# Token tiles 0 and 1 through w_v without their norm, the factor put on v's rows

## The chip, the cores and the metric

The kernel runs on one core of one Trainium2 chip. The metric is the device time of one execution in microseconds (us). The core's engines are TensorE (PE: matmuls and transposes), VectorE (DVE), ScalarE (ACT), GpSimd (POOL) and SyncE (SP, which issues most DMAs). Each engine works through its own queue in order; semaphores order them among each other.

## The reference

One residual block over 1024 tokens of width 1024, in float32:

```python
def rmsnorm(x, g):
    y = xf * lax.rsqrt(jnp.mean(xf * xf, axis=-1, keepdims=True) + RMS_EPS)
    return (y * g.astype(jnp.float32)).astype(x.dtype)

h = rmsnorm(x, norm_mix_pre[l])
m = mixer(h, w_in[l], b_f[l], conv_w[l], w_branch[l], w_out[l])
x = x + rmsnorm(m, norm_mix_post[l])
h = rmsnorm(x, norm_ffn_pre[l])
f = swiglu(h, w_gate_up[l], w_down[l])
x = x + rmsnorm(f, norm_ffn_post[l])
```

The mixer projects h by w_in onto q, k, v, a forget logit and the inputs of a gated convolution and of two gates. It merges a short convolution with an attention that has a bias from the forget gates, and projects by w_out. The change concerns h = rmsnorm(x) and v = h · w_v, with the eight forget logits as eight more columns of w_v. The factor 1/sqrt(mean(x²) + eps) of the norm is one number per token, so per row of h and of v; the gain g is one number per column of h.

## The kernel before

The tokens are cut into eight tiles of 128. For each tile the kernel loads x, takes the sum of squares on ACT, the factor on POOL (`rms_scale`: an addition `va` and a power `r1`), and scales x (`hn`). PE turns the tile by eight 128x128 transposes into two PSUM tiles `tp` (tag `mm`, four buffers). The turned columns are split into a rounded high part and a low remainder (`hB11h`, `hB11l` and so on): ACT copies to the rounded type, DVE subtracts. A product is three matmuls, high by high, high by low, low by high, so v of a tile is 2 column halves x 8 k-slices x 3 = 48 matmuls of 260 columns into PSUM (`pv`, two buffers). `v_out` copies v out of PSUM on ACT and stores it by a POOL DMA.

The projections behind it are products of the Strassen kind on a 2x2 cut of h. Its four blocks are `hB11` (tokens 0 to 511, k-slices 0 to 3), `hB21` (same tokens, k-slices 4 to 7), `B12` and `hB22` (tokens 512 to 1023). Tiles 4 to 7 therefore make four sums each on DVE (`t12`, `t34`) from their own turned columns and those of tiles 0 to 3, which are kept unsplit in `hraw`; two 1024-column splits (`hT12`, `hT34`) follow.

In the head of the kernel all engines keep program order (`strict`), so the order is written out by hand (lines 425 to 531). Between the first loads and the first products PE runs matmuls on a tile of zeros (`spins`). Tiles 0 and 1 (`Scaled`) are normed without the gain, turned, and get the gain as a column factor `gcol` when `hraw` is written; their v accumulates slice by slice as the slices of w_v arrive (`Parts`, with `wv_high` and `wv_low` splitting a slice). From tile 2 on the gain is in the norm (`gm`). From line 533 on tiles 2 to 7 run in a loop, whose order on DVE, ACT and POOL is set by a scheduler. DMA issues are part of their queue's order too: SP issues the loads of x and w_v, each of x's three buffers is loaded again when its last reader is done.

Of the kernel before, what the change touches and what calls it, by code (L numbers as in the profile page):

```python
# [10 lines left out]
F32 = mybir.dt.float32  # L11
# [35 lines left out]
def block_kernel(  # L47
# [58 lines left out]
    def f32(ap):  # L106
        return ap.bitcast(F32)
# [10 lines left out]
    def copy(o, a):  # L118
        nc.scalar.activation(o, a, AF.Copy)
# [42 lines left out]
    nc.vector.memset(ones, 1.0)  # L162
# [8 lines left out]
    pad(stat, 112, "pad_s")  # L171
# [6 lines left out]
    def st_tile(name, w=1):  # L178
        return stat.tile([P, w], F32, tag=name, name=name)
# [57 lines left out]
    strict[0] = engines  # L237
    gm = ax.tile([P, D], F32, name="gm")
# [9 lines left out]
    nc.scalar.activation(warm, ones[:, 0:1], AF.Square)  # L248
# [11 lines left out]
    zero = ap.tile([P, 4, P], F32R, tag="b12h", name="zero", bufs=2)  # L260
    nc.vector.memset(f32(zero), 0.0)
# [22 lines left out]
    def norm_sum(st):  # L284

        xt = xq.popleft()
        hn = ap.tile([P, D], F32, tag="hn", name="hn", bufs=2)
        ssq = st_tile("ssq")
        nc.scalar.activation(hn, xt, AF.Square, scale=ROOT, accum_out=ssq)
        return xt, hn, ssq  # L290

    def norm_rest(st, xt, hn, rs):

        nc.vector.scalar_tensor_tensor(hn, xt, rs, gm, op0=ALU.mult, op1=ALU.mult)
        if st + 3 < ST:
            xq.append(load_x(st + 3))
        return hn
# [5 lines left out]
    def turned(hn):  # L303

        tps = []
        for q in range(2):
            tp = psa.tile([P, 4, P], F32, tag="mm", name="tp")
            for k in range(4):
                kt = 4 * q + k
                nc.tensor.transpose(tp[:, k, :], hn[:, kt * P : (kt + 1) * P], ident)  # L310
            tps.append(tp)
        return tps
# [3 lines left out]
    class Scaled:  # L316


        def __init__(self, st):
            self.ss = slice(st * P, (st + 1) * P)  # L320
            self.ops = [tuple(t[:, :, self.ss] for t in b) for b in (hB11, hB21)]

# [3 lines left out]
        def turn(self, hn):  # L326
            self.tps = turned(hn)
# [97 lines left out]
    xt = xq.popleft()  # L425
    hn = ap.tile([P, D], F32, tag="hn", name="hn", bufs=2)
    s2, part = st_tile("s2", 2), st_tile("nm")
    for n, c in enumerate((n1, n2)):
        nc.scalar.activation(
            hn[:, c], xt[:, c], AF.Square, scale=ROOT, accum_out=s2[:, n : n + 1]  # L430
        )
        if n == 0:
            nc.vector.tensor_scalar(part, s2[:, 0:1], EPS, None, op0=ALU.add)
    rs0 = rms_scale(s2[:, 1:2], part)
    nc.vector.tensor_scalar(hn[:, n1], xt[:, n1], rs0, None, op0=ALU.mult)
    nc.scalar.activation(hn[:, n2], xt[:, n2], AF.Identity, scale=rs0)
    nc.vector.tensor_copy(gcol, gps)
    xq.append(load_x(3))
    t0, t1 = Scaled(0), Scaled(1)
    t0.turn(hn)  # L440
    spins(4)
    xt1, hn1, ssq1 = norm_sum(1)
    wv_high(0)
    t0.scale(0)
    t0.high(0)

    def between():
        t0.scale(1)
        t0.low(0)

    rs1 = rms_scale(ssq1, between=between)
    v0, v1 = Parts(t0.ops), Parts(t1.ops)
    v0.run("hh", 0)
    spins(1)
    wv_high(1)
    v0.run("hh", 1)
    v0.run("lh", 0, 1)
    t0.high(1)
    nc.vector.tensor_scalar(hn1[:, n1], xt1[:, n1], rs1, None, op0=ALU.mult)
    nc.scalar.activation(hn1[:, n2], xt1[:, n2], AF.Identity, scale=rs1)  # L460
    xq.append(load_x(4))
    spins(1)
    t1.turn(hn1)
    wv_low(0)
    wv_high(2)
    v0.run("hh", 2)
    v0.run("lh", 2)
    v0.run("hl", 0)
    wv_high(3)
    t0.low(1)  # L470
    v0.run("hh", 3)
    v0.run("lh", 3)
    wv_high(4)
    t1.scale(0)
    t1.high(0)
    wv_low(1)
    v0.run("hh", 4)
    v0.run("lh", 4)
    v0.run("hl", 1)
    wv_high(5)  # L480
    t1.low(0)
    t1.scale(1)
    v1.run("hh", *range(4))
    v1.run("lh", *range(4))
    wv_high(6)
    wv_low(2)
    t1.high(1)
    v1.run("hl", 0, 1)
    t1.low(1)
    wv_high(7)  # L490
    wv_low(3)
    for k in (2,):
        v0.run("hl", k)
        v1.run("hl", k)
    v0.run("hh", 5)
    v0.run("lh", 5)
    xt2, hn, ssq2 = norm_sum(2)
    v0.run("hl", 3)
    v1.run("hl", 3)
    wv_low(4)  # L500
    v0.run("hh", 6)
    v0.run("lh", 6)
    sum3 = norm_sum(3)

    def between():
        for k in (5, 6, 7):
            wv_low(k)

    rs2 = rms_scale(ssq2, between=between)
    v1.run("hh", 4, 5)  # L510
    v1.run("lh", 4, 5)
    v0.run("hl", 4)
    v1.run("hl", 4)
    norm_rest(2, xt2, hn, rs2)
    v0.run("hh", 7)
    v0.run("lh", 7)
    v1.run("hh", 6)
    v1.run("lh", 6)
    v0.run("hl", 5, 6, 7)
    rs3 = rms_scale(sum3[2])  # L520
    v_out(0, v0.pv)
    v1.run("hh", 7)
    v1.run("lh", 7)
    v1.run("hl", 5, 6)
    cur = turn(2, hn)
# [1793 lines left out]
```

## Time and profile before

| what | value |
|---|---|
| median of 3 runs | 1318.18 us (1317.93 to 1319.31) |
| profiled execution | 1319.89 us |
| span of the profiled execution | 1318.0 us |
| PE busy | 1308.8 us (99% of the span) |
| DVE busy | 917.2 us (70%) |
| ACT busy | 555.8 us (42%) |
| POOL busy | 185.6 us (14%) |

Times in the profile count from the start of the span. The chain that ended last is followed back from the last instruction through what released each step; its pieces say where the time of the end is made. A row of the timeline has its start, its length, the engine, the line, and the operation with its tiles; the brackets behind it say how long the engine had been idle and what ended that. A matmul's length is modelled and includes its way through the array, so the distance between starts says how fast PE goes. Most operations are recorded on one helper line (L76), so groups are told apart by tiles.

### The profile page before, as it was taken

How to read it: one execution, taken by the hardware profiler on the slowest of the kernel's cores; microseconds unless marked ns; L12 is line 12 of the kernel's file. 1: busy time of each engine (PE TensorE's matmuls, PEld its weight loads, DVE VectorE, ACT ScalarE, POOL GpSimd, SP SyncE). 2: the span in 40 equal slices, each digit the busy share in tenths (PEclk: the TensorE clock that was granted, in tenths of full speed). 3: DMA queues.
4: the chain of work that ended last, by engine and by line, in shares of the span. 5: the costliest groups of instructions: out<-in, count | busy, mean ns of one | idle time of the engine just before them, and what ended most of it. 6: DMA issues, size and time to landing. Idle time of an engine off the chain costs nothing.

```text
span 1318.0 us, 17686 instructions
## 1 busy us (share of the span) xinstructions
PE 1308.8 (99%) x6695; PEld 1089.3 (83%) x6695; DVE 917.2 (70%) x1313; ACT 555.8 (42%) x869; POOL 185.6 (14%) x347
## 2 busy tenths in 40 slices
PE   9999999999999999999999999999999999999998
PEld 8988888888888888888888888888888888888886
DVE  6883768776756866676667788866766666677674
ACT  6631323243355766513678432222322234344451
POOL 3101001012112212011223112111001110000001
PEclk9999999999999999999999999999999999999999
DMA  6352423556536445674476565533323337966551
GB/s 225 90 160 88 141 61 119 183 194 195 196 128 206 154 138 166 210 257 132 131 231 227 174 198 193 176 120 104 99 86 115 110 106 271 364 217 192 159 169 64
DMA packets 168389, 215.71 MB, mean 164 GB/s; under 512 B 11480, under 2 KB 113952, under 8 KB 168304
## 3 DMA queue, kind: packets, MB, share of 16 engines
q1 hardware_dynamic: 146352, 141.40, 34.5%
q0 software_dynamic: 21952, 73.19, 15.3%
q8 instruction: 52, 0.85, 0.3%
q14 instruction: 33, 0.27, 0.1%
HBM read 153.41 MB, written 61.15 MB: 163 GB/s over the span
## 4 chain that ended last, share of the span: by engine, by line
PE 96%; ACT 1%; DVE 1%; DMA 1%; issue 1%; POOL 0%; DVEq 0%; POOLq 0%; SPq 0%; ACTq 0%
PE b L76 61%; PE pd L76 16%; PE pv L76 4%; PE pbb L76 3%; PE pba L76 3%; PE po L76 2%; PE tps L76 2%; PE sp L76 2%; PE tp L76 1%; PE ma L76 1%; PE mb L76 1%; DMA raw<-in_w_gate_up_dram 0%; ACT raw L76 0%; DMA xt<-in_x_dram 0%; DVE x L76 0%
## 5 line engine op out<-in xcount | busy, mean ns | idle before, releaser
L76 DVE TENSOR_TENSOR c<-c,b 128x512 f32<-128x512 f32 x215 | 146.8, 683 | 96.9 <-PE b L76 87.4
L76 DVE TENSOR_TENSOR lo<-raw,hi 128x1024 fp32r<-128x1024 f32 (+1 forms) x91 | 109.7, 1205 | 81.2 <-PE b L76 65.7
L76 ACT ACTIVATE hi<-raw 128x1024 fp32r<-128x1024 f32 (+1 forms) x98 | 99.7, 1017 | 102.0 <-PE b L76 68.5
L76 ACT ACTIVATE hi<-sx 128x1024 fp32r<-128x1024 f32 x44 | 46.8, 1063 | 207.2 <-PE b L76 181.3
L76 DVE TENSOR_TENSOR lo<-sx,hi 128x1024 fp32r<-128x1024 f32 x44 | 53.8, 1223 | 39.6 <-PE b L76 37.9
L76 PE MATMUL b<-w12h,lo 128*128 128x512 f32 x208 | 80.9, 389 | 0.0
L76 PE MATMUL b<-w12h,hi 128*128 128x512 f32 x204 | 79.4, 389 | 0.0
L76 PE MATMUL b<-w12l,hi 128*128 128x512 f32 x204 | 79.4, 389 | 0.0
L76 PE MATMUL b<-hh,hi 128*128 128x512 f32 x176 | 69.0, 392 | 0.0
L76 PE MATMUL b<-hh,lo 128*128 128x512 f32 x176 | 68.5, 389 | 0.0
L76 PE MATMUL b<-hl,hi 128*128 128x512 f32 x176 | 68.5, 389 | 0.0
L76 DVE TENSOR_TENSOR sx<-raw 128x512 f32<-128x512 f32 x78 | 53.6, 687 | 20.0 <-DMA raw<-in_w_in_dram 10.3
L76 PE MATMUL b<-w,s4h 128*128 128x512 f32 x208 | 64.0, 389 | 0.0
L76 PE MATMUL pd<-hi,lo 128*128 128x512 f32 x160 | 62.3, 389 | 0.0
L76 PE MATMUL pd<-hi 128*128 128x512 f32 x160 | 61.9, 390 | 0.0
L76 PE MATMUL pd<-ghi 128*128 128x512 f32 x148 | 57.6, 389 | 0.0
L76 PE MATMUL pd<-ghi,glo 128*128 128x512 f32 x148 | 57.6, 389 | 0.0
L76 PE MATMUL pd<-glo,ghi 128*128 128x512 f32 x148 | 57.6, 389 | 0.0
L76 POOL DMA_DIRECT2D a_dramA<-um x33 | 17.9, 541 | 276.6 <-DVE um L76 275.8
L76 PE MATMUL b<-hT34h,hi 128*128 128x512 f32 x136 | 53.0, 390 | 0.4 <-DVE c L76 0.4
L76 PE MATMUL b<-hT34h,lo 128*128 128x512 f32 x136 | 52.9, 389 | 0.0
L76 PE MATMUL b<-hT12h,hi 128*128 128x512 f32 x136 | 52.9, 389 | 0.0
(451 smaller groups left out, 3572.8 us busy)
## 6 DMA issues: line engine op xcount, KB each, us to landing
raw<-in_w_gate_up_dram SPq DMA_DIRECT2D x52, 512.0 KB, 3.8
raw<-in_w_in_dram SPq DMA_DIRECT2D x35, 512.0 KB, 3.8
a_dramS<-um POOLq DMA_DIRECT2D x44, 256.0 KB, 3.1
a_dramA<-um POOLq DMA_DIRECT2D x33, 256.0 KB, 2.6
sg<-sg_dram SPq DMA_DIRECT2D x32, 256.0 KB, 4.2
graw<-a_dramS SPq DMA_DIRECT2D x14, 512.0 KB, 4.3
sg_dram<-c POOLq DMA_DIRECT2D x24, 256.0 KB, 2.5
raw<-in_w_down_dram SPq DMA_DIRECT2D x11, 512.0 KB, 4.4
```

The lines of the kernel that those rows point to most:

```text
L76: ins = getattr(self.engine, name)(*args, **kw)
```

## The change

Tiles 0 and 1 are turned as they were loaded (`First`, in place of `Scaled`), the gain is put on with `gcol` as before, and the products with w_v are made from these columns, whose rows lack the norm's factor. The factor is put on when v is copied out of PSUM (`v_out(..., scale=firsts[t].rs)`). The squares of tiles 0 and 1 come later in the order, and the order of the head is written as a string of steps (`wh`, `wl`: high and low part of a slice of w_v; `x`, `s`, `h`, `l`: transposes, gain, high and low part of half a tile; `phh13`: high by high for tile 1, slice 3; `sq`, `pw`: square and power). `settle`, behind v of tile 2, puts the two factors on the columns of tiles 0 and 1 in `hraw` and splits them again for the projections: two diagonal matrices of the factors (POOL), one matmul with a tile of ones that spreads them over the partitions (PE), its copy (ACT), two multiplications over 4x256 columns (POOL), two roundings (ACT) and two remainders (DVE). Loads move too: w_v's slice 0 goes between the two halves of x0, all of w_v ahead of x of tile 2, the gain by ACT's queue, the forget bias at the start on POOL's.

```diff
-    def load_x(st):
+    def load_x(st, between=None):
         xt = ax.tile([P, D], F32, tag="x", name="xt", bufs=3)
         rows = x2d[st * P : (st + 1) * P, :]
-        for c in (n1, n2) if st == 0 else (slice(0, D),):
+        for c in (n1, n2) if between else (slice(0, D),):
             nc.sync.dma_start(xt[:, c], rows[:, c])
+            if between and c is n1:
+                between()
         return xt
...
-    xq = deque([load_x(0)])
-    nc.sync.dma_start(g8, norm_mix_pre[0].rearrange("(k p) -> k p", p=P))
-    xq.append(load_x(1))
-    for k in range(8):
+    nc.scalar.dma_start(g8, norm_mix_pre[0].rearrange("(k p) -> k p", p=P))
+    nc.gpsimd.dma_start(bf, b_f[0].partition_broadcast(P))
+    xts = [load_x(0, load_wv), load_x(1)]
+    for k in range(7):
         load_wv()
-        if k == 4:
-            xq.append(load_x(2))
+    xq = {2: load_x(2)}
...
-    def v_out(st, pv):
+    def v_out(st, pv, **kw):
         vs = vs_tile()
-        copy(vs.rearrange("p (n c) -> p n c", n=2), pv[:, :, :hv])
+        nc.scalar.activation(
+            vs.rearrange("p (n c) -> p n c", n=2), pv[:, :, :hv], AF.Copy, **kw
+        )
...
+    def square(t):
+        if t < 2:
+            firsts[t].square()
+        else:
+            later[t] = norm_sum(t)
+        if t == 0:
+            nc.sync.dma_start(gm, norm_mix_pre[0].partition_broadcast(P))
+            xq[3] = load_x(3)
+        if t == 1:
+            xq[4] = load_x(4)
...
+    firsts[0].turn(0)
+    nc.tensor.transpose(gps, g8, ident[:KT, :KT])
+    spins(1)
     nc.vector.tensor_copy(gcol, gps)
...
+    steps_(
+        "s00 wh0 h00 x01 wl0 phh00 s01 phl00 l00 h01 x10 plh00 s10 wh1 x11 l01 h10 "
...
+        "plh15 wh7 pw2 phl04 phl14 phh06 plh06 sq3 sq1"
+    )
...
+    v_out(0, parts[0].pv, scale=firsts[0].rs)
...
+    def settle():
+
+        z = z_tile("rs")
+        dg = z[:, : 2 * P].rearrange("p (t c) -> p t c", t=2)
+        rb = z[:, 2 * P : 4 * P]
+        for t, f in enumerate(firsts):
+            nc.gpsimd.tensor_scalar(dg[:, t, :], ident, f.rs, None, op0=ALU.mult)
+        rp = psa.tile([P, 4, P], F32, tag="mm", name="rp")[:, :2, :]
+        nc.tensor.matmul(flat_(rp), ones, flat_(dg), start=True, stop=True)
+        copy(rb, flat_(rp))
+        both = slice(0, 2 * P)
+        for q, (hh, hl) in enumerate((hB11, hB21)):
+            raw = hraw[:, 4 * q : 4 * q + 4, both]
+            nc.gpsimd.tensor_tensor(
+                raw, raw, rb.unsqueeze(1).broadcast_to([P, 4, 2 * P]), op=ALU.mult
+            )
+            split(hh[:, :, both], hl[:, :, both], raw)
+
...
             v_out(2, v2.pv)
+            settle()
```

PE's queue at the very start, before (`spin` is a matmul on zeros, `gps` the turned gain, `tp` the transposes of x, `pv` the products with w_v):

```order
L76 MATMUL spin<-zero 128x512 x7
L76 MATMUL gps<-ident,gm 128x8
L76 MATMUL spin<-zero 128x512 x3
L76 MATMUL tp<-ident,hn 128x128 x8
L76 MATMUL spin<-zero 128x512 x4
L76 MATMUL pv<-wvh,hB11h 128x260 x2
L76 MATMUL spin<-zero 128x512
L76 MATMUL pv<-wvh,hB11h 128x260 x2
L76 MATMUL pv<-wvh,hB11l 128x260 x4
L76 MATMUL spin<-zero 128x512
L76 MATMUL tp<-ident,hn 128x128 x8
```

And PE's queue at the same place now:

```order
L76 MATMUL spin<-zero 128x512 x4
L76 MATMUL tp<-ident,xt 128x128 x4
L76 MATMUL gps<-ident,gm 128x8
L76 MATMUL spin<-zero 128x512
L76 MATMUL tp<-ident,xt 128x128 x4
L76 MATMUL pv<-wvh,hB11h 128x260 x2
L76 MATMUL pv<-wvl,hB11h 128x260 x2
L76 MATMUL tp<-ident,xt 128x128 x4
L76 MATMUL pv<-wvh,hB11l 128x260 x2
L76 MATMUL tp<-ident,xt 128x128 x4
L76 MATMUL pv<-wvh,hB11h 128x260 x2
```

The transposes read `xt`, as loaded, in four groups of four, with five spins in place of sixteen.

POOL's queue behind v of tile 2, before (`va` and `r` are a norm's addition and power, here tile 6's):

```order
L76 DMA v_dram<-vs 128x512 [waits Activation_49]
L76 TENSOR_SCALAR va<-ssq 128x1 [waits Activation_49]
L76 TENSOR_TENSOR r_643<-va,power 128x1 [waits DVE_49,Pool_49]
L76 DMA v_dram<-vs 128x512 [waits Activation_49]
L76 TENSOR_SCALAR va<-ssq 128x1 [waits Activation_49]
```

The same place now:

```order
L76 DMA v_dram<-vs 128x512 [waits Activation_49]
L76 TENSOR_TENSOR hraw<-hraw,rs 128x4x256 [waits Activation_49]
L76 TENSOR_TENSOR hraw<-hraw,rs 128x4x256
L76 TENSOR_SCALAR va<-ssq 128x1 [waits Activation_49]
L76 TENSOR_TENSOR r_635<-va,power 128x1 [waits Pool_49]
L76 DMA v_dram<-vs 128x512 [waits Activation_49]
```

The two multiplications of `settle` stand between v 2's store and the factor of tile 6.

DVE's queue from the norm of tile 6 (`hn` from `xt`) to the sums of tile 5 that read the transposes (`tp`), before:

```order
L76 SCALAR_TENSOR_TENSOR hn<-xt,r_643,gm 128x1024 [waits DVE_49,DMAHW2_49,Activation_49,Pool_49]
L76 TENSOR_TENSOR t_699<-b_549,hraw 128x512 [waits Activation_49]
...
L76 SCALAR_TENSOR_TENSOR hn<-xt,r_732,gm 128x1024 [waits DMAHW3_49,Activation_49,Pool_49]
L76 TENSOR_TENSOR t_798<-b_630,hraw 128x512 [waits Activation_49]
L76 TENSOR_TENSOR t_798<-tp,t_798 128x512 [waits DVE_49]
L76 TENSOR_TENSOR t_799<-tp,b_630 128x512
```

And now:

```order
L76 SCALAR_TENSOR_TENSOR hn<-xt,r_635,gm 128x1024 [waits DVE_49,DMAHW2_49,Activation_49,Pool_49]
L76 TENSOR_TENSOR hB11l<-hraw,hB11h 128x4x256 [waits Activation_49]
L76 TENSOR_TENSOR hB21l<-hraw,hB21h 128x4x256 [waits Activation_49]
L76 TENSOR_TENSOR t_691<-b_541,hraw 128x512 [waits Activation_49]
...
L76 TENSOR_TENSOR t_790<-tp,t_790 128x512 [waits DVE_49]
L76 TENSOR_TENSOR b12l<-tp,b12h 128x512 [waits Activation_49]
L76 TENSOR_TENSOR hB22l<-tp,hB22h 128x4x128 [waits Activation_49]
L76 TENSOR_TENSOR t_791<-tp,b_622 128x512
```

The two remainders of `settle` come behind tile 6's norm and ahead of all sums, and two remainders of tile 6 stand ahead of tile 5's sum. From the first split of a projection weight on, every engine's order is that of before.

## Rows read from the trace of the kernel before

**Rows 1.** The page, section 4: the chain by engine, share of the span.

```profile
PE 96%; ACT 1%; DVE 1%; DMA 1%; issue 1%; POOL 0%; DVEq 0%; POOLq 0%; SPq 0%; ACTq 0%
```

**Rows 2.** The chain of waits, 0 to 70 us: start, length, what.

```profile
1.17 3.29 DMA xt<-in_x_dram
...
6.82 1.97 PE tp L76 x8
...
24.48 2.91 PE pv L76 x22
...
31.39 0.87 PE tp L76 x8
...
38.88 5.75 PE pv L76 x48
...
63.62 6.58 PE b L76 x29
```

**Rows 3.** Timeline, PE: start, length, engine, line, operation, tiles.

```profile
1.58 3.35 PE L76 MATMUL spin<-zero 128*128 128x512 f32 x7 [1.58 <-DVE zero L76]
...
10.73 0.49 PE L76 MATMUL spin<-zero 128*128 128x512 f32 x1
11.06 0.40 PE L76 MATMUL pv<-wvh,hB11h 128*128 128x260 f32 x2
```

**Rows 4.** Timeline, SP's queue of DMA issues.

```profile
2.46 2.00 SPq L76 DMA_DIRECT2D wr<-in_w_in_dram  x4
...
5.21 0.71 SPq L76 DMA_DIRECT2D xt<-in_x_dram  x1
...
9.40 1.94 SPq L76 DMA_DIRECT2D xt<-in_x_dram  x2
```

**Rows 5.** DMA issues of 2.4:2.9, 5.1:5.9 and 20:22 us: KB, us to landing.

```profile
wr<-in_w_in_dram SPq DMA_DIRECT2D x1, 260.0 KB, 5.5
...
xt<-in_x_dram SPq DMA_DIRECT2D x1, 512.0 KB, 6.7
...
xt<-in_x_dram SPq DMA_DIRECT2D x1, 512.0 KB, 3.5
```

**Rows 6.** Timeline, ACT and DVE, 6.9 to 9.5 us.

```profile
6.91 1.04 ACT L76 ACTIVATE hn<-xt 128x1024 f32<-128x1024 f32 x1
...
8.70 0.63 ACT L76 ACTIVATE hB11h<-hraw 128x512 fp32r<-128x512 f32 x1
...
8.83 0.69 DVE L76 TENSOR_TENSOR hraw<-tp,gcol 128x512 f32<-128x512 f32 x1 [0.16 <-PE tp L76]
9.24 0.62 ACT L76 ACTIVATE wvh<-wr 128x520 fp32r<-128x520 f32 x1
...
9.44 0.68 DVE L76 TENSOR_TENSOR hB11l<-hraw,hB11h 128x512 fp32r<-128x512 f32 x1
```

**Rows 7.** Groups by line, POOL: count, busy us, mean ns, idle before.

```profile
L76 POOL TENSOR_TENSOR rows<-rows,mask 128x128 f32<-128x128 f32 x32 | 14.5, 457 | 62.2 <-DVE nm L76 56.3 <-DMA rows<-c_dram 5.8
```

**Rows 8.** Timeline, POOL, 32 to 35 us.

```profile
32.38 0.63 POOL L76 DMA_DIRECT2D v_dram<-vs  x1 [1.43 <-ACT vs L76]
34.19 0.22 POOL L76 TENSOR_SCALAR va<-ssq 128x1 f32<-128x1 f32 x1 [1.18 <-ACT hn L76]
```

**Rows 9.** Timeline, DVE and PE, 31 to 52 us.

```profile
31.23 1.03 PE L76 MATMUL tp<-ident,hn 128*128 128x128 f32 x8
...
35.09 1.29 DVE L76 SCALAR_TENSOR_TENSOR hn<-xt,r,gm 128x1024 f32<-128x1024 f32 x1 [1.20 <-POOL r L76]
...
40.03 1.23 DVE L76 TENSOR_TENSOR hT34l<-t,hT34h 128x1024 fp32r<-128x1024 f32 x1
...
43.49 1.28 DVE L76 SCALAR_TENSOR_TENSOR hn<-xt,r,gm 128x1024 f32<-128x1024 f32 x1 [0.96 <-POOL r L76]
...
46.02 0.68 DVE L76 TENSOR_TENSOR t<-tp,b 128x512 f32<-128x512 f32 x1
...
51.10 1.04 PE L76 MATMUL tp<-ident,hn 128*128 128x128 f32 x8
```

More of the change, by code (lines that the diff above doesn't have):

```diff
@@ L237, in block_kernel @@
     strict[0] = engines
+    zero = ap.tile([P, 4, P], F32R, tag="b12h", name="zero", bufs=2)
+    nc.vector.memset(f32(zero), 0.0)
+    nc.vector.memset(ones, 1.0)
     gm = ax.tile([P, D], F32, name="gm")
     g8 = gm[:KT, :P]
[L240 to L243 removed]
+    nc.scalar.dma_start(g8, norm_mix_pre[0].rearrange("(k p) -> k p", p=P))
+    nc.gpsimd.dma_start(bf, b_f[0].partition_broadcast(P))
+    xts = [load_x(0, load_wv), load_x(1)]
+    for k in range(7):
         load_wv()
[L245 to L246 removed]
+    xq = {2: load_x(2)}
     warm = st_tile("warm")
[L248 removed]
+    nc.scalar.activation(warm, f32(zero)[:, 0, 0:1], AF.Square)
     wvh = av.tile([P, KT, VF], F32R, name="wvh")
@@ L270, in spins @@
             )
-    spins(7)
+    spins(4)
     gps = psa.tile([P, 4, P], F32, tag="mm", name="gps")[:, 0, :KT]
-    nc.tensor.transpose(gps, g8, ident[:KT, :KT])
-    nc.sync.dma_start(gm, norm_mix_pre[0].partition_broadcast(P))
-    spins(3)
     def wv_high(k):
@@ L295, in norm_rest @@
         if st + 3 < ST:
[L296 removed]
+            xq[st + 3] = load_x(st + 3)
         return hn
@@ L301, in norm, with flat_, turned @@
         return norm_rest(st, xt, hn, rms_scale(ssq))
[L303 to L312, printed above, removed]
+    def flat_(t):
+        return t.rearrange("p a b -> p (a b)")
+    def turned(hn, q):
+        tp = psa.tile([P, 4, P], F32, tag="mm", name="tp")
+        for k in range(4):
+            kt = 4 * q + k
+            nc.tensor.transpose(tp[:, k, :], hn[:, kt * P : (kt + 1) * P], ident)
+        return tp
     hraw = av.tile([P, KT, NC], F32, name="hraw")
-    class Scaled:
+    class First:
         def __init__(self, st):
@@ L321, in __init__, with turn @@
             self.ops = [tuple(t[:, :, self.ss] for t in b) for b in (hB11, hB21)]
+            self.tps, self.xt = {}, xts[st]
         def raw(self, q):
             return hraw[:, 4 * q : 4 * q + 4, self.ss]
-        def turn(self, hn):
-            self.tps = turned(hn)
+        def turn(self, q):
+            self.tps[q] = turned(self.xt, q)
         def scale(self, q):
@@ L337, in low, with square, root @@
             sub(self.ops[q][1], self.raw(q), f32(self.ops[q][0]))
+        def square(self):
+            self.ssq = st_tile("ssq")
+            nc.scalar.activation(
+                self.xt, self.xt, AF.Square, scale=ROOT, accum_out=self.ssq
+            )
+        def root(self):
+            self.rs = rms_scale(self.ssq)
     def turn(st, hn):
         ss = slice(st % 4 * P, (st % 4 + 1) * P)
-        tps = turned(hn)
+        tps = [turned(hn, q) for q in range(2)]
         if st < 4:
@@ L422, in v_out @@
             flast.clear()
[L425 to L435, printed above, removed]
@@ L436, in block_kernel @@
-    nc.scalar.activation(hn[:, n2], xt[:, n2], AF.Identity, scale=rs0)
-    nc.vector.tensor_copy(gcol, gps)
[L438 to L525, printed above, removed]
@@ L526, in block_kernel, with root @@
-    v1.run("hl", 7)
+    firsts = [First(t) for t in range(2)]
+    later, norms = {}, {}
+    def square(t):
[8 more added lines that the diff above has]
+            xq[4] = load_x(4)
+    def root(t):
+        if t < 2:
+            firsts[t].root()
+        else:
+            norms[t] = rms_scale(later[t][2])
@@ new lines, in step, with steps_ @@
+    def step(o):
+        n = int(o[-1])
+        if o[:2] in ("wh", "wl", "sq", "pw"):
+            return dict(wh=wv_high, wl=wv_low, sq=square, pw=root)[o[:2]](n)
+        if o[0] == "x":
+            return firsts[int(o[1])].turn(n)
+        if o[0] == "p":
+            return parts[int(o[3])].run(o[1:3], n)
+        getattr(firsts[int(o[1])], dict(s="scale", h="high", l="low")[o[0]])(n)
+    def steps_(row):
+        for o in row.split():
+            step(o)
+    firsts[0].turn(0)
+    nc.tensor.transpose(gps, g8, ident[:KT, :KT])
@@ L527, in block_kernel @@
+    spins(1)
+    nc.vector.tensor_copy(gcol, gps)
+    parts = [Parts(f.ops) for f in firsts]
+    steps_(
[5 rows of a table added]
+    )
+    hn = norm_rest(2, *later[2][:2], norms[2])
+    steps_("phh16 plh16 phl05 phl15 phh07 pw3 wl7 pw1")
+    later[2] = turn(2, hn)
+    hn = norm_rest(3, *later[3][:2], norms[3])
+    steps_("plh07 phl06 phl07")
+    v_out(0, parts[0].pv, scale=firsts[0].rs)
+    steps_("phh17 plh17 phl16 phl17")
+    v_out(1, parts[1].pv, scale=firsts[1].rs)
+    cur = later[2]
     strict[0] = ("vector", "scalar", "gpsimd")
-    nc.gpsimd.dma_start(bf, b_f[0].partition_broadcast(P))
```

11 lines of the change are left out of this document (4 added, 7 removed), and 3 rows, old and new, of the table parts.

## The prediction

> **What bounds the kernel now.** The page's chain comes first: TensorE (PE) carries 96% of the chain that ended last [rows 1]. So a change of a few instructions counts only where PE has nothing to do, and the chain's first 70 us show where that is [rows 2]. PE's first useful work, the transposes of token tile 0, starts at 6.82 us. Ahead of it stand the load of x, whose second half lands at 1.17 + 3.29 = 4.46, and then 2.36 us of norm (square, power, scaling). v of tile 2 starts at 24.48, the transposes of tile 4 at 31.39, and the projections at 63.62. From 24.48 on PE runs without a gap: a v tile is 48 matmuls of 0.12 (5.75 us for 48), a turned tile 8 transposes (0.87). Hence, if nothing else becomes late, the end moves by as much as v of tile 2 moves.
>
> Two things slow the head besides the norm. The first is the clock: the transposes at 6.82 took 1.97 us for eight, those at 31.39 only 0.87. The granted clock is listed as full for all of the head, but such durations are those of 1.2 and of 2.4 GHz. The rise shows in the filler matmul of 512 columns at 10.73, whose successor starts 0.33 later, between the 0.43 of half and the 0.22 of full clock [rows 3]: the clock rose near 11.0. PE had worked unbroken since 6.82; through the fillers from 1.58 on it stayed low. The second is the loads: w_v's slice 0 is issued at 2.46 and lands 5.5 later, x of tile 2 is issued at 5.21 and lands 6.7 later [rows 4, 5].
>
> **The change part by part: the head.** The squares, the power and the scaling of tiles 0 and 1 go from ahead of their transposes to behind them. What then paces PE is the loads. By bytes in order of issue, 0.52 MB were there at 4.46 and 1.32 MB (w_v slice 0 the last) at 7.96, so 0.23 MB/us; x of tile 2 closes 2.90 MB at 11.9, so 0.40 MB/us from there [rows 2, 4, 5]. For the new order of issue that gives, as an estimate, 3.3 for x0's first half, 4.5 for w_v 0, 5.6 for x0's second half, 7.9 for x1, 8.6, 9.3 and 9.9 for w_v 1 to 3, 10.6 to 12.6 for w_v 4 to 7, and 14.0 for x2.
>
> PE at half clock takes 0.22 for a transpose or a 260-column matmul, twice what it takes at full: four transposes at 3.3, four at 5.6 to 6.5, four matmuls to 7.3, x1's first four transposes at 7.9 to 8.8, two matmuls, x1's last four to 10.1, then only matmuls. The left operand comes in time: VectorE (DVE) does one 512-column scaling or remainder every 0.61 (8.83 to 9.44), ScalarE (ACT) one rounding every 0.54 (8.70 to 9.24) [rows 6], so tile 1's first rounded piece is there at 10.3 and its matmuls start at 10.9. PE is unbroken from 7.9, 1.1 later than before, and I place the rise of the clock 1.1 later too, at 12.0. By then 16 of the 96 matmuls of tiles 0 and 1 are done; 80 at 0.12 and tile 2's transposes (0.87) bring v of tile 2 to 12.1 + 9.6 + 0.9 = 22.6.
>
> Does another engine end later? ACT takes the square of tile 0 behind w_v 5, at 13.7 to 14.8 (1.04 as the row at 6.91); x of tile 3, which was issued from 9.40 on, now waits for that buffer and lands 3.5 later, as a later tile of x did [rows 4 to 6], at 18.4. Squares 3 and 1 then end at 20.6, and three ACT pieces of 0.54 (tile 2's two roundings and v 0's copy out, which frees the PSUM that v 2 writes) end at 22.2: 0.4 ahead of PE. So v of tile 2 starts at 22.6 for 24.48: **1.9 us gained**.
>
> **The settling behind v of tile 2.** PE gets one float32 matmul of 256 columns. The nearest rows, f32 transposes, have 0.11 for 128 columns, so 0.22 for 256, and twice that if it goes through the array in more passes; with less than nothing excluded, since it is added work, I take **0.4 lost**. ACT's two roundings and DVE's two remainders of 1024 columns are weighed below.
>
> POOL (GpSimd) and DVE are the hard part. POOL gets two multiplications of 1024 columns, behind v 2's DMA issue and ahead of the power for tile 6. No row of before shows one. Bounds: not less than the 128-column one, 0.46; not more than eight times that, 3.66. With the one-column operation, 0.22, as the fixed part, the other 0.24 over 127 columns give 1.87 ns each and 2.1 for 1024 [rows 7, 8]; I take 2.1, from the nearest row. The GPSIMD Engine Reference of the Trainium skill (section 3.1, Elementwise, side-by-side cycle accounting) states 4497 ns for a sum over 2048 float32 columns; half of it, 2.25, is an estimate that no run here shows, and by it the wait below would be 0.3 longer.
>
> Now times from Z, the end of v of tile 2, 31.23 before. Before, DVE started the norm of tile 6 at 35.09, Z + 3.9, having waited 1.20 for POOL's power, and ended tile 5's sum t<-tp,b at 46.70, 11.6 later, with 0.96 of waiting inside [rows 9]. After: v 2's copy out ends at Z + 0.9, POOL issues v 2's DMA 0.3 later in 0.63 [rows 8], so the multiplications run from Z + 1.85 to 6.1, the power is there at 7.0, and the norm starts 3.1 later than before. DVE works in order: every sum stands behind that norm. Up to tile 5's sum it now has two 1024-column remainders more (1.2 each, as at 40.03) and tile 6's two of 512 columns (0.61 each), which stood behind the sum; the 0.96 goes: 11.6 + 2.4 + 1.2 + 0.1 - 1.0 = 14.3. So the sum ends at Z + 21.3.
>
> Who waits for it: transposes use four PSUM buffers, two a tile, so tile 7's take over those of tile 5, and this sum is the last reader of one. Before, tile 7's transposes started at 51.10 [rows 9], Z + 19.9, 4.4 us behind the sum. Now PE is there at Z + 0.4 + 19.9 = 20.3 and waits **1.0**. What is late next is the first raw weight of the projections, whose load waits for tile 7's sum; by the same count it comes some 0.4 ahead of its use, and I cost it at nothing.
>
> **Sum.** -1.9 + 0.4 + 1.0 = -0.5 us. The profiled execution took 1319.89 us (span 1318.0, 1.9 around it), so 1319.4; it was 1.7 above the median of the runs, 1318.18. On the median it is **1317.7 us**. About 0.2%, 2.6 us, is what a measurement of this kernel can tell from no change: I forecast no change that can be told.
>
> **Rivals.** First, the clock rises late. PE now has gaps at 4.9 to 5.6 and 7.3 to 7.9, only 5 filler matmuls instead of 16, and transposes among its matmuls until 10.1. If the rise comes as much behind 10.1 as it came behind 6.82, it is at 14.2, 2.2 later, which is 1.1 us of work at full clock: +0.6, 1318.8. Against it: before, that stretch began with eight transposes too [rows 2]. The Trainium skill (TensorE: Matmul & The Clock Gate, Part 4: PE-mode transpose) says that the full clock does not engage for transposes; the rows at 6.82 and 31.39 differ from it, as the later eight ran at more than twice the rate, but none shows a rise among transposes, and by that rule the first rival is the case.
>
> Second, on the other side: POOL's multiplications are dear. Each 0.1 us more in one is 0.2 us more of wait at tile 7, so from 2.35 us each on the kernel is slower than before; at the upper bound of 3.66 the sum is -0.5 + 3.1 = +2.6, 1320.8, and with the late clock past it. For it: no row of POOL's arithmetic is longer than 128 columns, so the slope hangs on one pair of short rows. Against it: half of the short row is fixed cost.
>
> Third, the settling is hidden: at 1.6 us or less per multiplication PE never waits for the sum. Then -1.5, and with x1 landing 0.9 earlier (it has 4 KB less ahead of it, and w_v 0's landing bounds it from above only) -2.4: 1315.8 to 1316.7. Beyond -2.6 it needs loads at 0.40 MB/us from the start.
>
> That the change doesn't do what it says is possible in one way: v of tile 2 at 24 or later, because ACT waits for x of tile 3 with all behind it; that is +1 us.
>
> **Chances.** The forecast, within 1 us of 1317.7: 0.40. Late clock alone, or ACT waiting for x3: 0.22, of which 0.03 pass +2.6. Dear multiplications: 0.18, of which 0.11 pass +2.6 with or without the clock. Hidden settling: 0.20, of which 0.14 pass -2.6. So faster by over 0.2%: 0.14; within: 0.72; slower: 0.14. The range, 1315.4 to 1320.6, runs from a hidden settling with early loads to nearly the upper bound of the multiplications; the likeliest case by itself is 1316.7 to 1318.7.
>
> **What would show it.** Right: v of tile 2 starting between 22.2 and 23, rows at half clock until near 12, POOL's 1024-column rows near 2.1, DVE idle some 4 us ahead of tile 6's norm, and PE idle about 1 us ahead of tile 7's transposes. Wrong: v of tile 2 before 21 or after 24, no wait at tile 7, or a wait at the first projections instead.

## The result, and the profile after

The changed kernel takes 1323.15 us (median of 6 runs, 1322.27 to 1323.84) against 1318.57 of the kernel before (6 runs, 1317.93 to 1319.31): ratio 1.0034, 95% interval 1.0021 to 1.0047. It is slower by 4.6 us of median. Forecast were 1317.7 and a range up to 1320.6, so the time lies outside what was forecast. The profiled execution took 1323.09 us, its span is 1321.1, 3.1 longer than the span before.

The chain of waits of the changed kernel, its first 70 us (start, length, what; against [rows 2]):

```profile
2.12 7.72 DMA xt<-in_x_dram
9.84 0.04 issue
9.89 1.11 PE tp L76 x4
...
12.29 9.56 PE pv L76 x76
...
32.83 4.76 POOL hraw L76 x2
...
52.92 0.66 PE tp L76 x4
53.57 11.48 PE pv L76 x96
65.05 7.04 PE b L76 x31
```

x of tile 1, issued at 2.12, lands at 9.84. The forecast had 7.9. TensorE (PE) works without a gap only from there, and the projections start at 65.05, 1.43 later than before. PE's timeline of the changed kernel, with the idle time ahead of a row in brackets (against [rows 3, 9]):

```profile
6.58 1.12 PE L76 MATMUL tp<-ident,xt 128*128 128x128 f32 x4 [1.03 <-DMA xt<-in_x_dram]
...
9.89 1.11 PE L76 MATMUL tp<-ident,xt 128*128 128x128 f32 x4 [1.33 <-DMA xt<-in_x_dram]
...
12.52 0.64 PE L76 MATMUL pv<-wvh,hB11l 128*128 128x260 f32 x2
12.96 0.50 PE L76 MATMUL pv<-wvh,hB11h 128*128 128x260 f32 x2
13.29 0.40 PE L76 MATMUL pv<-wvl,hB11h 128*128 128x260 f32 x2
13.53 0.40 PE L76 MATMUL pv<-wvh,hB11h 128*128 128x260 f32 x2
...
24.28 1.23 PE L76 MATMUL pv<-wvh,hB11h 128*128 128x260 f32 x8
...
31.02 0.59 PE L76 MATMUL rp<-rs,ones 128*128 128x256 f32 x2
...
51.32 0.60 PE L76 MATMUL tp<-ident,hn 128*128 128x128 f32 x4
52.92 0.66 PE L76 MATMUL tp<-ident,hn 128*128 128x128 f32 x4 [1.00 <-ACT b L76]
```

x of tile 0's second half, which the forecast had at 5.6, lets its transposes start only at 6.58. Four transposes at 9.89 still take 1.11, which is 1.2 GHz; the distance between matmuls goes from 0.22 to 0.12 near 13 (two from 12.52 to 12.96, two from 13.29 to 13.53). v of tile 2 starts at 24.28: 0.2 earlier than before, where 1.9 were forecast. The float32 matmul takes 0.43 (31.02 to 31.45), and PE stands 1.00 in the middle of tile 7's transposes: the first four run at 51.32, the other four at 52.92. The settling on POOL, the norm of tile 6 and the sum of tile 5 on DVE (against [rows 7 to 9]), and the copy on ACT that ended PE's wait:

```profile
32.83 4.75 POOL L76 TENSOR_TENSOR hraw<-hraw,rs 128x1024 f32<-128x1024 f32 x2
38.57 1.28 DVE L76 SCALAR_TENSOR_TENSOR hn<-xt,r,gm 128x1024 f32<-128x1024 f32 x1 [4.57 <-POOL r L76]
...
52.28 0.58 ACT L76 ACTIVATE b<-tp 128x512 f32<-128x512 f32 x1
...
52.40 0.68 DVE L76 TENSOR_TENSOR t<-tp,b 128x512 f32<-128x512 f32 x1
```

POOL takes 2.38 for each multiplication, and DVE stands 4.57 for tile 6's power. From the projections to 679 us both kernels run in step, 1.4 to 1.5 apart. Then another 1.6 are lost in one place, which the prediction does not mention: the first products of the feed-forward part, computed ahead. ACT's copies of them in the kernel before:

```profile
682.58 0.60 ACT L76 ACTIVATE c<-b 128x512 f32<-128x512 f32 x1
...
688.48 0.60 ACT L76 ACTIVATE c<-b 128x512 f32<-128x512 f32 x1 [3.96 <-DMA pre_dram<-c]
```

and in the changed kernel:

```profile
684.06 0.60 ACT L76 ACTIVATE c<-b 128x512 f32<-128x512 f32 x1
...
691.47 0.60 ACT L76 ACTIVATE c<-b 128x512 f32<-128x512 f32 x1 [5.39 <-DMA pre_dram<-c]
```

The second copy reuses the tile of the first, so it waits for the first one's store (256 KB, beside 2 MB of weight loads). Before, that store took 4.8 from issue to landing, now 6.3. ACT works in order, so all of it stands behind the copy, and PE's transposes that stood at 698.70, which need a tile from ACT, come at 701.73.

### The profile page after: what moved, and what is told of

Same layout as the page of the kernel before. It is cut to its first block, busy times and chain, and to the rows that moved or that the text cites. A ratio compares the mean times of both kernels' runs of the same rounds, so it can differ in the third digit from the quotient of the medians.

```text
span 1321.1 us, 17667 instructions
## 1 busy us (share of the span) xinstructions
PE 1308.0 (99%) x6686; PEld 1087.7 (82%) x6686; DVE 918.5 (70%) x1312; ACT 556.5 (42%) x868; POOL 191.2 (14%) x351
## 4 chain that ended last, share of the span: by engine, by line
PE 94%; ACT 2%; issue 1%; DMA 1%; POOL 1%; DVE 1%; SPq 0%; DVEq 0%; POOLq 0%; ACTq 0%
PE b L76 61%; PE pd L76 16%; PE pba L76 3%; PE pbb L76 3%; PE po L76 2%; PE tps L76 2%; PE sp L76 2%; PE pv L76 2%; PE ma L76 1%; PE tp L76 1%; PE mb L76 1%; DMA xt<-in_x_dram 1%; DMA pre_dram<-c 0%; POOL hraw L76 0%; POOL r L76 0%
## 5 line engine op out<-in xcount | busy, mean ns | idle before, releaser
L76 PE MATMUL b<-hT34l,hi 128*128 128x512 f32 x136 | 52.9, 389 | 0.0
```

The lines of the kernel that those rows point to most:

```text
L76: ins = getattr(self.engine, name)(*args, **kw)
```

## The experiments

Times are medians, each set against runs of the kernel before on the same chip (1318.7 to 1319.3).

### The forget bias late

```diff
-    nc.gpsimd.dma_start(bf, b_f[0].partition_broadcast(P))
     xts = [load_x(0, load_wv), load_x(1)]
...
+    nc.gpsimd.dma_start(bf, b_f[0].partition_broadcast(P))
     v_out(1, parts[1].pv, scale=firsts[1].rs)
```

> The changed kernel, with one load moved back to where the kernel before has it: the forget bias, 32 bytes to each of 128 partitions, on POOL's queue behind v of tile 0 and no longer at the start. Theory A, these many small pieces hold up the loads: the transfer rate, 67 GB/s from 5 to 6 us in the changed kernel, is back at 250 or more, x of tile 1 lands 0.9 earlier than 9.84, and v of tile 2 starts at 23.4 instead of 24.28; the time falls by 0.9 us. Theory B, the slices of w_v that are issued ahead of and beside x of tile 1 hold it up: nothing moves, x of tile 1 at 9.8 and v of tile 2 at 24.3.

The transfer rates (last column, GB/s) of the changed kernel by microsecond:

```profile
4.00:5.00 1.00, 1.00 (x5) 0.65 (x4) 0.14 (x1) 0.59 (x1) 0.00 (x0) 1.00 0.67 192
5.00:6.00 1.00, 0.55 (x1) 0.04 (x1) 0.97 (x3) 0.26 (x2) 0.00 (x0) 1.00 0.61 67
```

and with the bias late:

```profile
4.00:5.00 1.00, 1.00 (x5) 0.64 (x3) 0.17 (x1) 0.64 (x1) 0.00 (x0) 1.00 0.95 289
5.00:6.00 1.00, 0.83 (x3) 0.33 (x3) 0.98 (x2) 0.25 (x1) 0.00 (x0) 1.00 0.98 335
```

Theory A holds: x of tile 1 is turned at 7.55 without a wait, and v of tile 2 starts at 22.04, 2.2 earlier, more than expected. In time less of it comes out: 1322.13, 2.8 above the kernel before on the same chip, where the changed kernel is 4.3 to 4.6 above; the ratio, 1.0026 (1.0015 to 1.0036), has an interval that overlaps the changed kernel's. The bias, now issued at 23.10, lands 5.4 later, DVE stands 1.3 for it ahead of tile 3's remainders, PE's wait at tile 7 grows to 1.8, and the projections start at 64.33. Near 690 us the store takes 6.8, and from the first product with w12 near 601 us to the first with hh near 742 PE takes 143.0, 2.0 more than in the kernel before.

### The forget bias early, in the kernel before

The bias's load moves to the start of POOL's queue, as in the change; nothing else.

```diff
+    nc.gpsimd.dma_start(bf, b_f[0].partition_broadcast(P))
     xq = deque([load_x(0)])
...
-    nc.gpsimd.dma_start(bf, b_f[0].partition_broadcast(P))
     hn = norm_rest(3, *sum3[:2], rs3)
```

> The kernel before, with one thing of the change alone: the forget bias loaded at the start on POOL's queue. Theory A: its small pieces take the loads' engines near 5 to 6 us, where the rate falls from 295 GB/s to below 150, x of tile 1 and the slices of w_v come 0.7 to 1.2 later, and v of tile 2 starts at 25.0 to 25.7 instead of 24.48; 0.5 to 1.2 us slower. Rival: the kernel before has slack in its loads, because its norms pace it, and nothing changes (within 0.2 at v of tile 2) although the rate falls.

1322.72, ratio 1.0025 (1.0014 to 1.0035): this one line of the change makes the kernel before 3.6 us slower. The rates of the kernel before as it was:

```profile
4.00:5.00 1.00, 1.00 (x4) 0.35 (x2) 0.15 (x1) 0.51 (x1) 0.00 (x0) 1.00 0.80 254
5.00:6.00 1.00, 1.00 (x3) 0.88 (x4) 0.00 (x0) 0.21 (x2) 0.61 (x2) 1.00 0.80 295
```

and with the bias early:

```profile
4.00:5.00 1.00, 1.00 (x4) 0.35 (x2) 0.15 (x1) 0.74 (x4) 0.15 (x1) 1.00 0.53 83
5.00:6.00 1.00, 1.00 (x3) 0.88 (x4) 0.17 (x1) 0.17 (x1) 0.71 (x2) 1.00 0.47 133
```

The rate falls in the same place, x of tile 1 lands at 9.64, and v of tile 2 starts at 27.55: the loss is larger than expected, since PE then stands 3.35 ahead of its first product, and tile 1's eight transposes behind it take 1.89, at half clock.

### The forget bias early, from ACT's queue

```diff
-    nc.gpsimd.dma_start(bf, b_f[0].partition_broadcast(P))
+    nc.scalar.dma_start(bf, b_f[0].partition_broadcast(P))
```

> The changed kernel with the forget bias still loaded at the start, but from ACT's queue behind the gain and no longer from POOL's. It parts two readings of the early load. Theory H, its many 32-byte pieces as such hold up the other loads: the rate from 4 to 6 us stays below 200 GB/s, x of tile 1 lands at 9 or later, and v of tile 2 starts near 24.3. Theory I, it is the way over POOL's queue: the rate stays near 300 from 4 to 6 us, x of tile 1 lands by 8.0, and v of tile 2 starts by 22.8.

```profile
3.00:4.00 1.00, 0.93 (x4) 0.45 (x3) 0.00 (x0) 0.23 (x2) 0.00 (x0) 1.00 1.06 207
4.00:5.00 1.00, 1.00 (x6) 0.65 (x4) 0.09 (x1) 0.11 (x1) 0.00 (x0) 1.00 0.29 55
5.00:6.00 1.00, 0.60 (x1) 0.09 (x1) 0.97 (x3) 0.69 (x2) 0.00 (x0) 1.00 0.85 286
```

In between: the rate still falls, to 55, but it is back by 5 us; x of tile 1 is turned at 8.79, and the time is 1321.90, ratio 1.0017 (1.0007 to 1.0027). So in these profiles the pieces cost on either queue, and more over POOL's.

### x of tile 1 ahead of w_v

```diff
-    xts = [load_x(0, load_wv), load_x(1)]
-    for k in range(7):
+    xts = [load_x(0, lambda: None), load_x(1)]
+    for k in range(8):
```

> The changed kernel, with both halves of x of tile 0 and x of tile 1 issued ahead of all of w_v. Theory B (the slices of w_v hold up x of tile 1): x of tile 1 lands near 7, as in the kernel before, slice 0 of w_v near 8, TensorE is unbroken from about 8, and v of tile 2 starts at 22.4 to 23.0, 1.3 to 1.9 earlier; the time falls by as much. Theory A (the small pieces of the forget bias hold up all loads): the low rate stays, x of tile 1 lands near 8 and slice 0 behind 9, and v of tile 2 stays within 0.5 of 24.3. A third outcome, TensorE early but v of tile 2 still at 24, would say that ACT, which waits for x of tile 3, sets its start.

Neither comes out whole: slice 0 of w_v landed only at 10.09, PE stood 4.90 for its first product, v of tile 2 started at 27.5, and the time is 1325.47, ratio 1.0045 (1.0033 to 1.0058). Theory B falls: the change was right to issue slice 0 early.

### The settling left out

```diff
             v_out(2, v2.pv)
-            settle()
```

> The changed kernel without the settling: the columns of tiles 0 and 1 go into the projections without the norm's factor, so the work behind v of tile 2 is that of the kernel before. Theory: the settling is worth what TensorE lost between v of tile 2 and the projections, 1.63 us (0.2 gained at v of tile 2, 1.43 lost at the first projection), so the projections start near 63.4. Two ways for the rest of the loss, 1.5 us that appear between 679 and 704 us, where ACT waits for the store of pre_dram 5.4 us instead of 4.0. Theory C, it hangs on when transfers meet there and comes and goes with the kernel: it may stay, and the time is then 1321.5. Theory D, it follows from the settling: it goes too, and the time is 1320.

1320.45, ratio 1.0010 (1.0001 to 1.0018). v of tile 2 starts at 24.41 and the projections at 63.55: 39.14 us between them instead of 40.77, so the settling is worth the 1.63 it was taken for. The store near 690 took 4.87, and no more was lost there than in the kernel before; that fits D, but a later run with the settling in, its multiplications on DVE, has a short store too (4.8), so it is no proof.

### The settling one tile later

```diff
             v_out(2, v2.pv)
-            settle()
...
             rest()
+            if st == 3:
+                settle()
```

> The changed kernel, with the settling called one tile later in program order, which puts POOL's two multiplications behind the power for tile 6 and DVE's two remainders behind tile 4's first sum. Theory: the loss before the projections is DVE's queue, which stands still 4.6 us for the power of tile 6 and so ends tile 5's sum 6.4 us later than before, too late for the transposes of tile 7. With the power ahead of the multiplications that idle time goes, TensorE does not wait at tile 7, and the projections start at 63.6 to 64.0 instead of 65.05: 1.0 to 1.4 us less. Rival: the work itself is too much, the wait only moves to tile 4's or tile 5's sum, because they need the settled columns, and the projections start at 65 or later.

1324.29, ratio 1.0037 (1.0024 to 1.0049): the rival. POOL's order put the multiplications behind v of tile 3's store as well, at 39.94 instead of 32.83; the sums of tiles 4 and 5 waited for them, PE stood 0.5 at tile 6's transposes and 1.5 at tile 7's, and the projections started at 66.8.

### The multiplications on DVE

```diff
-            nc.gpsimd.tensor_tensor(
+            nc.vector.tensor_tensor(
                 raw, raw, rb.unsqueeze(1).broadcast_to([P, 4, 2 * P]), op=ALU.mult
```

> The changed kernel, with the settling's two multiplications of 1024 columns on DVE instead of POOL. Theory: the settling costs what it does because POOL's 2 x 2.38 us stand ahead of the power for tile 6, for which DVE stands still 4.57 us. On DVE two such operations are 2 x 1.2 (as the remainders of 1024 columns), done while DVE would stand still, so tile 6's power comes near 35, the wait of 4.57 goes, TensorE does not wait at tile 7, and the projections start at 63.9 (24.3 for v of tile 2, 39.1 of work as in the kernel before, 0.4 for the float32 matmul) instead of 65.05: 1.1 us less. Rival: the settling is too much work for DVE, and the projections stay at 64.8 or later.

```profile
33.23 2.36 DVE L76 TENSOR_TENSOR hraw<-hraw,rs 128x1024 f32<-128x1024 f32 x2
...
38.98 1.28 DVE L76 SCALAR_TENSOR_TENSOR hn<-xt,r,gm 128x1024 f32<-128x1024 f32 x1
```

The mechanism holds: DVE does both in 2.36 and no longer stands for tile 6's power, PE does not wait at tile 7, and from v of tile 2 to the projections it takes 39.56 instead of 40.77. The absolute places were off, since v of tile 2 started 1.1 later (25.34), for a reason of the clock that the last section shows. 1321.30, ratio 1.0017 (1.0008 to 1.0026).

### Both mended

```diff
-    nc.gpsimd.dma_start(bf, b_f[0].partition_broadcast(P))
...
     xq = {2: load_x(2)}
+    nc.sync.dma_start(bf, b_f[0].partition_broadcast(P))
...
-            nc.gpsimd.tensor_tensor(
+            nc.vector.tensor_tensor(
```

> The changed kernel with both mended: the forget bias loaded by SP behind x of tile 2, and the settling's multiplications on DVE. If the two causes are right and add up, x of tile 1 lands by 7.6, v of tile 2 starts near 22.0 as with the late forget bias alone, and the projections at 61.6 to 62.4, 1.2 to 2.0 ahead of the kernel before (63.62). In time that is 2.7 to 3.4 us less than the changed kernel, and 1 to 2 us less than the kernel before unless the store near 690 us takes some of it back. Rival: with the head 2 us earlier something else is late ahead of the projections (the first raw weight, or DVE), and half of it is lost there.

v of tile 2 starts at 21.84, the projections at 61.40: the two causes add up. Of the 2.2 by which that is ahead of the kernel before, 0.3 are given back on the way and 0.9 near 690 (the store took 5.6), and the time is 1318.74, ratio 0.9998 (0.9989 to 1.0007).

### Both mended, x first

```diff
-    xts = [load_x(0, load_wv), load_x(1)]
+    xts = [load_x(0, lambda: None), load_x(1)]
-    for k in range(7):
+    for k in range(8):
```

> The changed kernel with the forget bias loaded behind x of tile 2 and the settling's multiplications on DVE, and with both halves of x of tile 0 and x of tile 1 issued ahead of all of w_v. It asks for the other thing that the change moved in the head, slice 0 of w_v between the halves of x of tile 0. In the run with x first and the forget bias at the start, that slice landed at 10.09 and v of tile 2 started at 27.5. If the small pieces did that, it lands by 8.3 now, and v of tile 2 starts within 0.7 of 21.8. If the order of issue did it, the slice lands at 9 or later and v of tile 2 starts at 23 or later.

Slice 0 lands at 7.66, so the bias had cost it 2.4; but PE still stands 3.05 for its first product and comes back at half clock, ACT is later, and v of tile 2 starts at 24.38. 1322.38, ratio 1.0025 (1.0014 to 1.0036). The order of issue counts for itself, in favour of the change's.

### The changed kernel again

> The changed kernel once more, unchanged, on the chip of the runs beside it. The head is to be as before: v of tile 2 at 24.3, the projections at 65.0. Theory C (the late loss is a matter of how transfers meet and varies from one execution to the next): ACT's wait for the store of pre_dram near 690 us is not 5.4 again but anywhere from 4 to 6, and the time varies with it by 1 to 2 us. Theory E (it belongs to this program): 5.4 again, within 0.3, and 1.5 us lost between 679 and 704 us.

The projections start at 65.07, within 0.02. The store took 6.1, ACT waited 5.1, and PE was 1.4 further behind at 742 us. So one and the same program has nearly the same late loss twice: this speaks for E, not C. One of its seven times, 1320.19, is 2 us under the rest (median 1323.41, ratio 1.0027, 1.0016 to 1.0038); what that execution was spared was not seen.

### The copy near 690 us into another tile

```diff
     def f_a(f):
         b1 = bank(psm, "b1")
         prod(b1, fw[f]["A11"], hb[B11], True)
-        p1 = t_(fp, "c21")
+        p1 = t_(fp, "c12" if f == 1 else "c21")
```

In the changed kernel:

> The changed kernel with one edit 600 us behind the change: the first half of the second column block that is computed ahead for the feed-forward part (the copy on ACT at 691.47) is put into the other tile tag c12, so that it no longer waits for the store of the first block's half to DRAM (pre_dram, 6.1 to 6.3 us here, 4.9 in the kernel before). Theory: the 1.4 to 1.5 us lost between 679 and 742 us come from that wait alone, behind which ACT's whole queue stands. ACT's idle time of 5.4 ahead of this copy falls below 1, the transposes that stood at 701.7 come at most 0.3 behind their place, and the loss between 679 and 742 us is 0 to 0.3: the time falls by 1.2 to 1.5 us. Rival: all transfers are slow there, and what waited for the store waits for a load of the weights or for the next store instead: 1 us or more stays lost.

The chain there (against the two copies above):

```profile
660.98 19.06 PE b L76 x84
680.05 1.75 PE tp L76 x16
681.80 19.09 PE b L76 x84
700.88 1.75 PE tp L76 x16
702.63 57.32 PE b L76 x252
```

PE is unbroken and ACT waits for no store. From the first product with w12 to the first with hh, PE takes 140.4 (602.89 to 743.28), where the kernel before took 141.0 (600.87 to 741.87) and the changed kernel 142.6 (602.35 to 744.91). 1321.97, ratio 1.0021 (1.0010 to 1.0031), 1.4 less than the changed kernel (1323.41): as the theory said, though the two intervals overlap and it is the profile that shows it.

In the kernel before:

> The kernel before with only the copy near 690 us put into c12. In the kernel before the wait was 4.0 us on ACT, but TensorE lost only 0.3 us by it (from 677.86 to 700.75 it had 22.6 us of work). Theory: 0.3 us faster at most, the same within measurement. Rival: if it is faster by 1 us or more, the wait costs the kernel before as much as the changed one in most executions, and the late loss of the changed kernel is no part of the difference between the two.

1318.42, ratio 0.9996 (0.9987 to 1.0005): no difference that can be told. PE takes 140.4 from w12 to hh here too, so the wait had cost the kernel before 0.6 in its profile.

With both mends:

> The changed kernel with the forget bias loaded behind x of tile 2, the settling's multiplications on DVE, and the copy near 690 us into c12. The projections start at 61.4 as without the last edit, 2.2 ahead of the kernel before. Theory: the 1.1 us that were given back near 690 us are kept, the span ends 2.0 to 2.5 us ahead of the kernel before, and the time is 1316.6 to 1317.2, 0.15 to 0.2% under the kernel before. Rival: the loss there is only put off, and the time stays within 0.5 us of 1318.7.

1318.27, ratio 0.9996 (0.9987 to 1.0004). Near 690 nothing is lost any more, but in this execution v of tile 2 started at 22.69, 1.47 of it waiting for ACT and so for x of tile 3: a loss stood in the head instead, and the time fits the rival.

### The kernel before again, twice

> The kernel before once more, unchanged, for its trace. Theory F: its profiled execution was one with a late clock. Its head rises to full clock near 5 to 6 us in most executions, as in the run with c12 alone, and then v of tile 2 starts at 23.3 and the projections at 62.4, 1.2 earlier than in the profiled one; that is what the changed kernel's difference of medians, 4.6 us, has more than the difference of the two profiles, 3.2. Theory G: the rise near 11 is the rule, and v of tile 2 starts at 24.4 again.

> The kernel before a third time, unchanged, for its trace: the same question as in the run before this one. Theory F: full clock by 6 us, v of tile 2 at 23.3. Theory G: full clock near 11, v of tile 2 at 24.4. Near 690 us TensorE again loses 0.3 us or less.

PE's timeline of the second:

```profile
1.58 3.35 PE L76 MATMUL spin<-zero 128*128 128x512 f32 x7 [1.58 <-DVE zero L76]
...
5.07 1.32 PE L76 MATMUL spin<-zero 128*128 128x512 f32 x3
6.47 1.10 PE L76 MATMUL tp<-ident,hn 128*128 128x128 f32 x8
```

Eight transposes at 6.47 take 1.10, where [rows 2] have 1.97: full clock from near 6. v of tile 2 starts at 23.61 and 23.44, with c12 alone at 23.27. So the clock is as theory F has it: three of four executions of this head rise early, and the profile from which I forecast was the fourth. Not all of the 0.9 to 1.2 is the clock's: tile 0's transposes also began earlier in the three, at 6.35 to 6.50 for 6.82. From there to v of tile 2 they took 16.9 to 17.1 where the fourth took 17.7. Against these three, with projections at 62.40 to 62.75, the kernel with both mends is only 1.0 to 1.4 ahead there, and not 2.2.

In time the early head shows in one of the two: they took 1318.80 (the second) and 1320.06 (the first), the forecast's own profile 1319.89. From 601 to 742 us the first takes 141.5, the second 140.9, the forecast's 141.0; behind 742 the first lost another 0.6.

### Fillers in the changed head

```diff
-        "s00 wh0 h00 x01 wl0 phh00 s01 phl00 l00 h01 x10 ...
+        "s00 wh0 h00"
+    )
+    spins(3)
+    steps_("x01 wl0 phh00 s01 phl00 l00 h01")
+    spins(4)
+    steps_(
+        "x10 ...
```

> The changed kernel with seven more filler matmuls of 512 columns on zeros in the two gaps of the head: three ahead of the second half of tile 0's transposes, four ahead of tile 1's. The loads and all else are as in the changed kernel, so x of tile 1 still lands at 9.6 to 9.9. Theory: the gaps of 1.0 to 1.3 us there keep the clock at half until 12.7 to 13; with them filled it is full by 9 in most executions, as in the kernel before, and the stretch from 9.9 to 12.9 is done in half the time: v of tile 2 starts at 22.7 to 23.2 instead of 24.3, 1.1 to 1.5 us faster. Rival: the clock rises where it did (near 13), v of tile 2 stays at 24.3, and nothing is gained.

In the profile the clock is full by 9 (tile 1's first transposes take 0.66 for four), v of tile 2 starts at 23.61, where it waits 0.43 for ACT, and the projections at 64.38, 0.7 earlier. The time does not follow: 1323.45, ratio 1.0033 (1.0022 to 1.0045). Whether the other executions had the early clock was not seen.

### All mends

```diff
+        "s00 wh0 h00 x01"
...
+    spins(3)
+    steps_("wl0 phh00 s01 phl00 l00 h01")
+    spins(2)
...
-        "... wl3 plh12 wh4 phh03 plh03 wh5 l11 phh13 plh13 sq0 phl02 wl4 "
+        "... wl3 plh12 sq0 wh4 phh03 plh03 wh5 l11 phh13 plh13 phl02 wl4 "
```

on top of the late bias, the multiplications on DVE and c12.

> The changed kernel with the forget bias behind x of tile 2, the multiplications on DVE, the copy near 690 us in c12, five fillers in the head's gaps (three behind the second half of tile 0's transposes, two ahead of tile 1's), and the square of tile 0 ahead of the roundings of w_v's slices 4 and 5, so that x of tile 3 is issued about 1 us earlier. Without the last two v of tile 2 started at 22.69, 1.47 of it waiting for ACT, which waited for x of tile 3. Theory: v of tile 2 starts at 21.2 to 21.9, the projections at 60.8 to 61.5, and the time is 1317.0 to 1317.6. Rival: slices 4 and 5 come too late for TensorE instead, and v of tile 2 stays at 22.5 or later.

```profile
20.02 3.04 PE pv L76 x24
...
28.48 0.43 PE rp L76 x2
...
49.65 11.49 PE pv L76 x96
61.14 5.00 PE b L76 x22
```

v of tile 2 starts at 21.58, the projections at 61.14, as expected. The time is 1317.71 (1316.48 to 1320.48), just above what was expected, against 1318.70: ratio 0.9993 (0.9984 to 1.0002). The median is 1.0 lower, which is no difference that can be told.

## Why the prediction was wrong

**The loads: the step that failed first.** "By bytes in order of issue" x of tile 1 was to land at 7.9; it landed at 9.84. That sum gave the forget bias no cost, being 4 KB. It cost some 2 us: with the bias late tile 1 is turned at 7.55 and v of tile 2 starts at 22.04, near the 22.6 of the forecast; ACT's copy that frees its PSUM ends at 21.99, so just in time. In the six executions with the changed kernel's head v of tile 2 starts between 24.28 and 25.34, in the three with only the bias moved in it between 21.84 and 22.69. The kernel before issues it at 24.1, where it landed 3.2 later, behind these loads; no row of the prediction could show what it does to them.

**The clock.** The rise was placed at 12.0 and came near 13; with the bias late it came near 11.0, so the delay came through the loads. The base failed too: [rows 3] show one execution with a rise at 11.0, and in three other executions v of tile 2 started 0.9 to 1.2 earlier. The sum took its gain of 1.9 from that one head, but put it on the median of all runs. This may be most of what the medians (4.6) differ by beyond the profiled executions (3.2), but it is not shown: of the two early heads without any edit only one was faster as a whole. The first rival, the late clock, is half true: the rise came 1.0 behind the forecast, among matmuls again, and half clock lasted through tile 1's transposes.

**The settling: right in its queues and its size, with luck in the last step.** 0.43 for the matmul (0.4 forecast), 2.38 for a multiplication (2.1), and 1.0 of waiting at tile 7 (1.0): 1.63 from v of tile 2 to the projections for 1.4. DVE stands 4.57 ahead of tile 6's norm, as named (some 4). But by the forecast's own rule, 0.2 of wait for each 0.1, multiplications of 2.38 make the wait 1.6. The sum it waits for did come that late: it starts at 52.40 and ends at 53.08. PE did not wait for it. Its second four transposes start at 52.92, released by ACT's copy b (52.28 and 0.58), which stood behind a rounding that had waited for DVE's sums, and the first four did not wait at all. So the path ran through DVE's late queue, as forecast, but the release was another, and the 1.0 agrees by luck. The third rival, a hidden settling, is out; 2.38 is just past the 2.35 from which the second, dear multiplications, counts. Half of the figure in the GPSIMD Engine Reference of the Trainium skill (section 3.1) was an estimate of 2.25, and the trace with 2.38 is nearer to that.

**"If nothing else becomes late, the end moves by as much as v of tile 2 moves."** Something did, by 1.6: the same program order met a longer store near 690, and the copy that waits for it took that time from PE. That the wait is the cause is shown by the profile with c12; why the store is longer in this program stays open. It took 6.1 and 6.3 here, and 5.9 to 6.8 in four other runs with the multiplications on POOL. It took 4.7 to 5.3 in three profiles of the kernel before, 4.8 to 5.6 with the multiplications on DVE, and 4.9 without the settling. A fifth run with them on POOL, x of tile 1 ahead of w_v, took 5.3, so the place of the multiplications alone does not explain it.

By the profiles, then: -0.2 for the head, +1.63 for the settling, +1.56 near 690, +0.1 elsewhere: 3.1.

The rival nearest the truth is the last one, v of tile 2 at 24 or later, but only by its number; its cause, ACT waiting for x of tile 3, held PE up only in runs with the loads mended or the clock's rise made earlier.

## What to carry to other kernels

Move no load to the start because it is small: 4 KB in 32-byte pieces cost the loads on the path 2 us, and one run with that line alone would have told. A forecast of 2 us from one profile needs a second profile of the same kernel first, since the head alone moved by 0.9 to 1.2 here from one execution to the next. And a wait in an engine's queue that costs little now (4.0 us at ACT, 0.6 of them lost on PE) can cost more with the next change.

## What the hardware showed that was not expected

The pieces of the forget bias: in the changed kernel's first 20 us POOL's queue has 32 packets at 2.4% of 16 engines, 7.7 us of engine time or 0.24 each, where SP's 3055 packets take 69.7%, or 0.07 each. The Trainium skill (DMA: Bandwidth & Descriptors, Why small descriptors are slow) gives each packet about three fixed cycles and each DMA operation 32 bytes of descriptor metadata; a loss of 2 us does not follow from that, and here the trace decides. From ACT's queue the same pieces took 0.4% or less, and the rate still fell to 55 GB/s, so engine time is not all of it. What is the rest stays open.

An early rise of the clock can be lost again. In the run with the multiplications on DVE, PE had full clock at 6.67 (four transposes in 0.66), then stood 2.1 for x of tile 1. The windows there show the granted clock in the third column from the right; it falls to 0.50, the lower level, while PE stands:

```profile
7.00:8.00 1.00, 0.81 (x8) 0.60 (x5) 0.63 (x2) 0.00 (x0) 0.00 (x0) 1.00 0.86 311
8.00:9.00 1.00, 0.00 (x0) 0.00 (x0) 0.66 (x2) 0.63 (x1) 0.00 (x0) 0.86 1.03 404
9.00:10.00 1.00, 0.11 (x1) 0.11 (x2) 0.00 (x0) 0.00 (x0) 0.00 (x0) 0.50 1.03 401
```

An early rise is worth nothing there: the transposes at 9.89 took 1.11, the distance between matmuls went back to 0.12 only near 15.5 (near 13 in the changed kernel), and v of tile 2 started at 25.34.
